# Another way to compute the modulation in the first loop of a transformer-layer kernel: scale columns with the weights as moving operand, shift and gate as VectorE dot products

## The chip, the cores and the metric

The kernel runs on one core of a Trainium2 chip. Its engines have instruction queues of their own and meet at semaphores: TensorE (PE in the profile, with PEld for the loading of its stationary operand), VectorE (DVE), ScalarE (ACT), GpSimd (POOL) and SyncE (SP), which issues most DMAs. The metric is the device time of one execution in microseconds. Three runs of the kernel before took 1252.56, 1253.64 and 1255.13 us; their median, 1253.64, is the time before.

## What is computed

One layer of a diffusion backbone over 512 latent and 256 context tokens with D = 1024: a half-step SwiGLU network, token mixing (attention and a chunked gating network side by side), and a second SwiGLU network. The change is in the first of the three. Cut down to what matters:

```python
def modulate(h, shift, scale):
    return h * (1 + scale) + shift

def swiglu(h, w1, w3, w2):
    return (jax.nn.silu(h @ w1) * (h @ w3)) @ w2

def ffn_sublayer(h_in, shift, scale, gate, norm_w, w1, w3, w2):
    h = modulate(rms_norm(h_in, norm_w), shift, scale)
    return h_in + 0.5 * gate * swiglu(h, w1, w3, w2)

mx = jnp.split((jax.nn.silu(c) @ w_ada + b_ada)[:, None, :], N_MOD, axis=-1)
mc = jnp.split((jax.nn.silu(c_ctx) @ w_ada + b_ada)[None, None, :], N_MOD, axis=-1)
x = ffn_sublayer(x, mx[0], mx[1], mx[2], norm1_w, ffn1_w1, ffn1_w3, ffn1_w2)
ctx = ffn_sublayer(ctx, mc[0], mc[1], mc[2], norm1_w, ffn1_w1, ffn1_w3, ffn1_w2)
```

`w_ada` is 1024 by 9216: nine vectors of 1024 (shift, scale, gate for each sublayer), for two conditions, `c` for latent tokens and `c_ctx` for context tokens.

## The kernel before

Everything is kept transposed: a tile has 128 features on its partitions and tokens in its columns. `x` is 8 blocks of 128 features by 768 tokens (two groups of 256 latent and 128 context tokens). To reach fp32 accuracy at the speed of the reduced type, each operand is split into a high and a low half (`split`, `operand`: ScalarE casts the high half, VectorE subtracts it for the low half), and each product is three matmuls, high by high, high by low, low by high (`mm3`).

**Head.** `x` is loaded, ScalarE squares it, VectorE adds up the squares, and a matmul with ones (L407) gives the sum over features, from which `r` and `v` make the reciprocal root (`rs`). Columns of `w_ada` come as `block` tiles, 1 MB each: shift and scale of 128 features. `ada_mm` (L219) multiplies them with `sc`, silu of the two conditions: the weights are the stationary operand, and two columns move. For each feature block `ada_first` runs 16 of these (8 for the scale, 8 for the shift), and `ada_fin` turns the result into `a` = (1 + scale) times the norm weight, and `s`, the shift.

**First loop, over the 8 feature blocks k.** For block k VectorE multiplies `x` by `a` and `rs` (`first_x`, into a short-lived tile `xa`), ScalarE adds the shift into `hh`, VectorE makes the low half `hl`, and TensorE adds block k to the first two f's (`NFIRST`) of the up projection: 12 matmuls of 512 latent columns (L373). The context part follows some steps behind (`first_ctx`, 12 matmuls of 256 columns, L429). In this loop `nc.ordered` is set and matmuls are pinned, so VectorE, ScalarE, GpSimd and TensorE run in the order of the code; elsewhere a scheduler sets the order, and instructions that are not pinned may be put between. Only two `block` buffers exist, so the load for step k+2 waits for a block to be read.

**Plain up projections, f = 2 to 5 (`NPLAIN1` = 6).** `up1` runs 96 matmuls of 384 columns per f (L125 to L127). After f = 2, 3 and 4, `ada_gate` computes gates as `ada_mm` does. Meanwhile GpSimd prepares the sums of token blocks that the next stage needs (`diff`, `less`, L648 to L654), out of the high and low halves; they are split into T2, T3 and T4 as the scheduler finds room, and T1, which takes the place of a block that the plain projections still read, last.

**f = 6 to 21 by a seven-product scheme (`Winograd`).** Per f, 84 matmuls instead of 96; GpSimd forms sums of weights, VectorE sums of products. Between its parts `ada_step` computes the remaining vectors of `w_ada`, now on VectorE: `ada_dot` multiplies a tile of 128 by 1024 with `cb`, the condition laid out along the columns on all partitions, and accumulates along the row. `cb` is loaded by two DMAs that broadcast (`cvec`) and passed through silu (L469). The down projections (`down`) of five chunks of f's are put in after f = 5, 6, 10, 14 and 18, and the sixth follows the stage.

Of the kernel before, what the change touches and what calls it, by code (L numbers as in the profile page):

```python
# [31 lines left out]
LAG = 2  # L32
NPLAIN1 = 6
NPLAIN2 = 2
BLOCKS = 2
RAWS = 3
OPS = 5
# [93 lines left out]
def layer_kernel(ctx: ExitStack, tc: tile.TileContext, xT, cvec, wfirst, wst, wada, wuq, wkpe, cols, wrope, vnw, rope, out):  # L131
# [27 lines left out]
    sc = const.tile([P, NK, 2], F32, name="sc")  # L159
    epsc = const.tile([P, 1], F32, name="epsc")  # L160
# [26 lines left out]
    gp = fctx.enter_context(tc.tile_pool(name="ffn1g", bufs=2))  # L187
    sctx = ExitStack()
# [10 lines left out]
    def first_units(k):  # L199
        r, rw = st.block(wada, k), st.raw()  # L200
        nc.sync.dma_start(rw[:, :W1], wfirst[k])
        return r, rw

    units = [first_units(0)]
    for k in range(0, NK, 4):
        load_x(k, 4, slice(256, 384))
    units.append(first_units(1))
# [7 lines left out]
    between = []  # L215

    def ada_mm(pt, r, later=False):
        for kt in range(NK):
            f = lambda kt=kt: pin(nc.tensor.matmul(pt, r[:, kt * P : kt * P + P], sc[:, kt, :], start=kt == 0, stop=kt == NK - 1))  # L219
            between.append(f) if later else f()  # L220

    def ada_dot(raw, c, which):
# [3 lines left out]
        nc.vector.scalar_tensor_tensor(  # L226
            out, raw, 1.0, cb[:, which, :], ALU.mult, ALU.mult,
            accum_out=acc[which][:, c : c + 1],
        )
# [92 lines left out]
    class SsqAcc:  # L322
# [4 lines left out]
        def add(self, dt, x0):  # L327
# [25 lines left out]
    def rstd_start(which, pt):  # L353
# [12 lines left out]
    class Mixed:  # L366


        def __init__(self):
            self.tensor = self  # L370

        def matmul(self, *a, **k):
            pin(nc.tensor.matmul(*a, **k))  # L373
# [28 lines left out]
    ada_first(units[0][0], 0)  # L402
    sa = None
    for k in range(NK):
        sa = add_sq(sa, k, square0(0, k), nc.vector)
    sumx = mm()
    pin(nc.tensor.matmul(sumx, ones, sa, start=True, stop=True))  # L407
# [975 lines left out]
```

## Time and profile before

| | before |
|---|---|
| median of three runs | 1253.64 us |
| profiled execution, own time | 1256.85 us |
| its span, first to last instruction | 1255.1 us |
| TensorE busy | 1200.2 us (96%) |
| VectorE busy | 911.1 us (73%) |
| ScalarE busy | 532.7 us (42%) |
| GpSimd busy | 474.8 us (38%) |
| mean granted TensorE clock | 0.974 |
| chain that ended last | PE 76%, DVE 12%, POOL 3%, ACT 3%, DMA 3%, issue 3% |

The profiled execution is one run, 3.2 us above the median of the three; times inside it are counted from the start of its span. A busy TensorE is not TensorE at its peak: a matmul that runs at half clock counts as busy for twice as long, and one of two columns as much as its weights take to load. The part of the program that the change touches ends at about 240 us. What lies behind it, up to 1255.1, is the rest of the first network, token mixing and the second network.

### The profile page before, as it was taken

To read this page: it belongs to the slowest core of one execution; us is meant where nothing else is said; L and a number is where in the kernel's file an instruction comes from. 1 tells how busy PE (TensorE), PEld (TensorE's weight loads), DVE (VectorE), ACT (ScalarE), POOL (GpSimd) and SP (SyncE) were. 2 spreads that over 40 slices of the span, in tenths; PEclk is the share of its full clock that TensorE was granted. 3 is DMA by queue.
4 is the path that set the end of the run, shared out by engine and by line. 5 is a ranking of instruction groups with operands and counts; after the bars stand their busy time and mean duration, and the time that the engine had idled before them with its cause. 6 is when DMAs were issued, how large, how long until landed. Compare 5 with 4: busy or idle time off the path is not lost.

```text
span 1255.1 us, 19295 instructions
## 1 busy us (share of the span) xinstructions
PE 1200.2 (96%) x7266; PEld 1134.5 (90%) x7266; DVE 911.1 (73%) x1607; ACT 532.7 (42%) x1057; POOL 474.8 (38%) x435
## 2 busy tenths in 40 slices
PE   6999899998999999999999999999789999999998
PEld 6888899998999999999978878998778989999997
DVE  3445426889896787876884697776998777778784
ACT  3233222323324324323654455997554444444442
POOL 0328701123213214231541762887573434343330
PEclk9889889999999999999998999999899999999999
DMA  7443232334362372433413311002304132413212
GB/s 256 140 151 110 74 127 80 118 97 147 132 216 103 102 229 74 135 130 101 134 55 114 95 57 51 2 1 66 103 35 134 68 135 68 134 69 135 84 51 84
DMA packets 36093, 131.69 MB, mean 105 GB/s; under 512 B 3744, under 2 KB 10656, under 8 KB 30368
## 3 DMA queue, kind: packets, MB, share of 16 engines
q1 hardware_dynamic: 35568, 129.35, 31.2%
q8 instruction: 57, 0.93, 0.3%
q10 hardware_dynamic: 432, 1.11, 0.3%
q14 instruction: 36, 0.29, 0.1%
HBM read 128.35 MB, written 2.10 MB: 104 GB/s over the span
## 4 chain that ended last, share of the span: by engine, by line
PE 76%; DVE 12%; POOL 3%; ACT 3%; DMA 3%; issue 3%; SPq 0%; DVEq 0%; POOLq 0%; ACTq 0%
PE mm L125 15%; PE mm L126 15%; PE mm L127 15%; PE big L125 8%; PE big L126 7%; PE big L127 7%; PE mm L219 4%; DVE opl L103 3%; PE big L373 2%; DVE junk L226 1%; DMA raw<-wst 1%; PE mm L1060 1%; DMA block<-wada 1%; DVE x L314 1%; PE mm L1075 1%
## 5 line engine op out<-in xcount | busy, mean ns | idle before, releaser
L102 ACT CAST oph<-block 128x512 fp32r<-128x512 f32 x216 | 133.9, 621 | 242.8 <-PE mm L126 159.6
L103 DVE TENSOR_TENSOR opl<-block,oph 128x512 fp32r<-128x512 f32 x216 | 190.9, 887 | 36.8 <-ACT oph L102 36.2
L125 PE MATMUL mm<-gh,oph 128*128 128x384 f32 (+2 forms) x532 | 186.9, 353 | 4.0 <-DVE x L314 2.8
L127 PE MATMUL mm<-gh,opl 128*128 128x384 f32 (+2 forms) x532 | 186.1, 352 | 1.4 <-DVE opl L103 1.4
L126 PE MATMUL mm<-gl,oph 128*128 128x384 f32 (+2 forms) x532 | 187.0, 351 | 0.0
L103 DVE TENSOR_TENSOR opl<-raw,oph 128x512 fp32r<-128x512 f32 x162 | 129.3, 804 | 51.4 <-ACT oph L102 51.2
L102 ACT CAST oph<-raw 128x512 fp32r<-128x512 f32 x162 | 98.6, 618 | 150.8 <-PE mm L126 72.3
L571 POOL TENSOR_TENSOR block<-block 128x512 f32<-128x512 f32 x36 | 48.9, 1358 | 243.3 <-DVE opl L103 243.3
L555 POOL TENSOR_TENSOR s<-block 128x512 f32<-128x512 f32 x36 | 54.6, 1518 | 159.3 <-DMA block<-wst 66.0
L125 PEld LDWEIGHTS mm<-gh,oph 128*128 128x128 f32 x532 | 99.9, 188 | 12.4 <-PE mm L127 2.7
L125 PE MATMUL big<-hh,oph 128*128 128x384 f32 (+1 forms) x288 | 99.3, 345 | 11.7 <-DVE sl L308 5.2
L127 PEld LDWEIGHTS mm<-gh,opl 128*128 128x128 f32 x532 | 99.8, 188 | 8.7 <-DVE opl L103 2.0
L126 PEld LDWEIGHTS mm<-gl,oph 128*128 128x128 f32 x532 | 99.9, 188 | 6.6
L127 PE MATMUL big<-hh,opl 128*128 128x384 f32 (+1 forms) x288 | 98.8, 343 | 0.7 <-DVE opl L103 0.7
L126 PE MATMUL big<-hl,oph 128*128 128x384 f32 (+1 forms) x288 | 98.7, 343 | 0.0
L570 POOL TENSOR_TENSOR block<-s,block 128x512 f32<-128x512 f32 x36 | 54.2, 1505 | 109.7 <-DVE opl L103 109.0
L314 DVE SCALAR_TENSOR_TENSOR x<-mm,g,x 128x256 f32<-128x256 f32 x206 | 76.4, 412 | 16.6 <-PE mm L127 16.6
L320 DVE SCALAR_TENSOR_TENSOR x<-mm,g,x 128x512 f32<-128x512 f32 x55 | 41.0, 749 | 49.9 <-PE mm L127 49.8
L125 PEld LDWEIGHTS big<-hh,oph 128*128 128x128 f32 x288 | 56.7, 197 | 13.3 <-DVE sl L308 6.3
L569 POOL TENSOR_TENSOR block<-block 128x512 f32<-128x512 f32 x36 | 57.5, 1599 | 2.6
L127 PEld LDWEIGHTS big<-hh,opl 128*128 128x128 f32 x288 | 56.2, 195 | 1.6 <-DVE opl L103 1.4
L126 PEld LDWEIGHTS big<-hl,oph 128*128 128x128 f32 x288 | 56.4, 196 | 0.1
(497 smaller groups left out, 3446.3 us busy)
## 6 DMA issues: line engine op xcount, KB each, us to landing
raw<-wst SPq DMA_DIRECT2D x86, 512.0 KB, 4.0
block<-wst SPq DMA_DIRECT2D x36, 1024.0 KB, 4.9
raw<-wada SPq DMA_DIRECT2D x56, 512.0 KB, 4.2
block<-wada SPq DMA_DIRECT2D x8, 1024.0 KB, 5.0
x<-xT SPq DMA_DIRECT2D x6, 512.0 KB, 6.6
raw<-wfirst SPq DMA_DIRECT2D x8, 256.0 KB, 3.8
out<-x SPq DMA_DIRECT2D x7, 256.0 KB, 2.1
cb<-cvec ACTq DMA_DIRECT2D x2, 512.0 KB, 6.7
```

The costliest lines, as they stand in the source:

```text
L102: self.nc.scalar.copy(dst[0], src)
L103: (eng or self.nc.vector).tensor_sub(dst[1], src, dst[0].bitcast(F32))
L125: nc.tensor.matmul(out, lh, rh, start=first, stop=False, skip_group_check=more)
L126: nc.tensor.matmul(out, lh, rl, start=False, stop=False, skip_group_check=more)
L127: nc.tensor.matmul(out, ll, rh, start=False, stop=last, skip_group_check=more)
L219: f = lambda kt=kt: pin(nc.tensor.matmul(pt, r[:, kt * P : kt * P + P], sc[:, kt, :], start=kt == 0, stop=kt == NK - 1))
L314: nc.vector.scalar_tensor_tensor(x[:, dt, s0 : s0 + sn], pt[:, o : o + sn], mod_g[i][which][:, dt : dt + 1], x[:, dt, s0 : s0 + sn], ALU.m ...
L320: nc.vector.scalar_tensor_tensor(lat(x, dt), two(pt), mod_g[i][0][:, dt : dt + 1], lat(x, dt), ALU.mult, ALU.add)
L555: nc.gpsimd.tensor_add(s1, q[2], q[3])
L569: nc.gpsimd.tensor_sub(q[2], q[0], q[2])
L570: nc.gpsimd.tensor_sub(q[0], s1, q[0])
L571: nc.gpsimd.tensor_sub(q[1], q[1], q[0])
```

## The change

1. **Condition by broadcast matmuls.** The loads of `cvec` go. Sixteen matmuls with `sc` broadcast as the stationary operand and the identity as the moving one lay the condition out along the columns in PSUM, and ScalarE copies it to `cb` (`put_cb`). Four more matmuls with ones (`WARM`) follow.
2. **Scale with moving weights.** `ada_row` makes `sc` (two columns) the stationary operand and moves the weights, 128 columns at a time: 8 matmuls give the scale as a row, ScalarE copies it (`row`), and `ada_col` turns it into a column with one matmul.
3. **Shift and gate as dots.** `ada_shift` computes the shift of each block by two `ada_dot`s (one for each condition), and the gates are done by `ada_step` after f = 2 and 3.
4. **A step ahead.** In step k the code prepares `x`, `hh` and `hl` of k+1 and the modulation of k+2. There is a third `block` buffer, in the pool of the loop, and the first steps of the context part are set by a table (`ctx_h`).
5. **Kept h.** `first_x` writes into `hf`, which holds all of h in fp32. The token-block differences are made of it, one subtraction each, on VectorE (L663 to L668), instead of `diff` and `less` on GpSimd.
6. **`NPLAIN1` from 6 to 4.** f = 4 and 5 move from the plain form to the seven-product one.
7. Smaller: epsilon is the bias of the reciprocal root and is added in the steps behind it, so that the instructions that added it to the squares go; `w_ada` is laid out in another way on the host; a scratch size is set.

```diff
-NPLAIN1 = 6
+NPLAIN1 = 4
+WARM = 4
...
+    def ada_row(r, d):
+        o = pa[0:2, (d % 2) * P : (d % 2) * P + P]
+        for kt in range(NK):
+            pin(nc.tensor.matmul(o, sc[:, kt, :], r[:, kt * P : kt * P + P], start=kt == 0, stop=kt == NK - 1))
+        row = sp.tile([2, P], F32, tag="row", name=f"row_{d}")
+        nc.scalar.copy(row, o)
+        return row
+
+    def ada_col(row, d):
+        o = pa[:, 256 + 2 * d : 258 + 2 * d]
+        pin(nc.tensor.matmul(o, row, ident[0:2, 0:2], start=True, stop=True))
         nc.vector.tensor_scalar(
-            pairs[0][1][:, d, :], pa[:, 16 + 2 * d : 18 + 2 * d], b1[:, NK + d : NK + d + 1],
-            col[:, COL_N1 + d : COL_N1 + d + 1], ALU.add, ALU.mult)
-        nc.vector.tensor_scalar_add(pairs[0][0][:, d, :], pa[:, 2 * d : 2 * d + 2], col[:, d : d + 1])
+            pairs[0][1][:, d, :], o, b1[:, NK + d : NK + d + 1], col[:, COL_N1 + d : COL_N1 + d + 1], ALU.add, ALU.mult)
+
+    def ada_shift(r, d, alone=False):
+        for which in range(2):
+            ada_dot(r[:, D:], d, which, accs[:, d, which : which + 1])
+            if alone:
+                nc.vector.tensor_add(mod_s[0][which][:, d : d + 1], accs[:, d, which : which + 1], col[:, d : d + 1])
+            yield
+        if not alone:
+            nc.vector.tensor_scalar_add(pairs[0][0][:, d, :], accs[:, d, :], col[:, d : d + 1])
...
+    def first_h(k, which):
+        sel = parts[which][0]
+        nc.scalar.activation(sel(hf, k), sel(hf, k), AF.Identity, bias=mod_s[0][which][:, k : k + 1])
+        nc.scalar.copy(sel(hh, k), sel(hf, k))
...
     pa = mm()
-    ada_first(units[0][0], 0)
+    bb = [big() for _ in range(2)]
+    for w in range(2):
+        for kt in range(NK):
+            pin(nc.tensor.matmul(bb[w][:, kt // 4, (kt % 4) * P : (kt % 4) * P + P], sc[:, kt, w : w + 1].to_broadcast([P, P]), ident,
+                                 start=kt % 4 == 0, stop=True, skip_group_check=True))
+    for i in range(WARM):
+        pin(nc.tensor.matmul(two(warm[:, :256]), ones, ones2, start=True, stop=True))
...
+    ctx_h = {2: (0, 1), 3: (2, 3), 4: (4,), 5: (5,), 6: (6, 7)}
     for k in range(NK):
...
+        later = k + 2 < NK
+        shift = ada_shift(units[k + 2][0], k + 2) if later else iter(())
+        if k + 1 < NK:
+            first_x(k + 1, 0)
+            ops[k + 1] = st.operand(units[k + 1][1][:, :W1])
+            first_h(k + 1, 0)
+            next(shift, None)
+            first_l(k + 1, 0)
...
         for i in range(2 * NFIRST):
...
+            first_mm(k, i)
+        if later:
+            row = ada_row(units[k + 2][0], k + 2)
+        next(shift, None)
...
     def after1(f):
-        if f < NPLAIN1 - 1:
-            for d in range(3 * (f - NFIRST), min(NK, 3 * (f - NFIRST) + 3)):
-                ada_gate(d)
+        if f < NPLAIN1:
+            for _ in range(4):
+                ada_step()
...
             for i in range(4):
...
+                b11, b12, b21, b22 = (half(k0, g0, i) for k0 in (0, 4) for g0 in (0, 384))
+                nc.vector.tensor_sub(tmps[i], b12, b11)
+                nc.vector.tensor_sub(b12, b22, b12)
+                split([b[:, i, :] for b in blocks["T3"]], b12)
+                nc.vector.tensor_sub(b22, b22, tmps[i])
+                split([b[:, i, :] for b in blocks["T2"]], b22)
+                nc.vector.tensor_sub(b21, b21, b22)
+                split([b[:, i, :] for b in blocks["T4"]], b21)
```

The order of the instructions shows what moves. On TensorE, at the program's start, before:

```order
L211 MATMUL mm_129<-ones 128x256 x3
L219 MATMUL mm_137<-sc,block_115 128x2 x16
L407 MATMUL mm_179<-sq_00_154,ones 128x512
L219 MATMUL mm_137<-sc,block_123 128x2 x16
L219 MATMUL mm_137<-sc,block_211 128x2 x16
L373 MATMUL big_207<-hh,oph_219 128x512
```

And TensorE at the same place in the changed program (the numbers stand for buffers; `sq_00` is the sum of squares, `big_150` and `big_152` the broadcast condition, block_120 and block_126 the first two blocks of weights):

```order
L215 MATMUL mm_140<-ones 128x256 x3
L391 MATMUL big_150<-ident,sc 128x128 x8
L391 MATMUL big_152<-ident,sc 128x128 x8
L394 MATMUL mm_140<-ones 128x256 x4
L402 MATMUL mm_199<-sq_00_173,ones 128x512
L253 MATMUL mm_148<-block_120,sc 2x128 x8
L260 MATMUL mm_148<-ident,row_212 128x2
L253 MATMUL mm_148<-block_126,sc 2x128 x8
L260 MATMUL mm_148<-ident,row_246 128x2
L441 MATMUL big_258<-hh,oph_225 128x512
```

The sum of squares no longer stands behind matmuls that read a block of weights, and the third block's have moved behind the first 12 matmuls of the loop. On VectorE, one step of the loop without a context part, before (`mm_137` holds the modulation, `xa_0_1` is `x` scaled in block 1):

```order
L57 TENSOR_SCALAR a_75<-mm_137,b_73,col 128x2
L57 TENSOR_SCALAR s_74<-mm_137,col 128x2
L57 SCALAR_TENSOR_TENSOR xa_0_1_274<-x,a_75,v_198 128x512
L57 TENSOR_TENSOR opl_279<-raw_126,oph_277 128x512
L57 SCALAR_TENSOR_TENSOR hl<-xa_0_1_274,s_74,hh 128x2x256
```

And VectorE in the changed program, the step k = 0, which prepares block 1 and the shift of block 2 (block_134):

```order
L57 TENSOR_SCALAR a_75<-mm_148,b_73,col 128x2
L57 SCALAR_TENSOR_TENSOR hfull<-x,a_75,v_202 128x2x256
L57 TENSOR_TENSOR opl_271<-raw_129,oph_269 128x512
L57 SCALAR_TENSOR_TENSOR junk_277,accs<-block_134,cb 128x1024
L57 TENSOR_TENSOR hl<-hfull,hh 128x2x256
L57 SCALAR_TENSOR_TENSOR junk_303,accs<-block_134,cb 128x1024
L57 TENSOR_SCALAR s_74<-accs,col 128x2
```

Two dots of 128 by 1024 have come in, one of them ahead of the low half `hl`. On VectorE again, in f = 2, where gate dots (`raw_995`, `raw_1004`) have been put among other work; `raw_1021` is the first half of f = 3's weights:

```order
L223 SCALAR_TENSOR_TENSOR junk_998,accc<-raw_995,cb 128x1024
L313 TENSOR_TENSOR sl_880<-big_776,sl_880 128x384
L223 SCALAR_TENSOR_TENSOR junk_1001,accx<-raw_995,cb 128x1024
L306 TENSOR_TENSOR gl_772<-sl_880,gh_770 128x384
L103 TENSOR_TENSOR opl_1026<-raw_1021,oph_1024 128x512
L223 SCALAR_TENSOR_TENSOR junk_1007,accc<-raw_1004,cb 128x1024
L103 TENSOR_TENSOR opl_1032<-raw_1021,oph_1030 128x512
```

The low halves of f = 3's operands stand behind six gate dots; before, no dot stood in this part of VectorE's queue.

More of the change, by code (lines that the diff above doesn't have):

```diff
@@ L130, in layer_kernel @@
 @with_exitstack
-def layer_kernel(ctx: ExitStack, tc: tile.TileContext, xT, cvec, wfirst, wst, wada, wuq, wkpe, cols, wrope, vnw, rope, out):
+def layer_kernel(ctx: ExitStack, tc: tile.TileContext, xT, wfirst, wst, wada, wuq, wkpe, cols, wrope, vnw, rope, out):
     nc = Core(tc)
@@ L199, in first_units @@
     def first_units(k):
-        r, rw = st.block(wada, k), st.raw()
+        r, rw = st.block(wada, k, sp if k % 3 == 2 else None), st.raw()
         nc.sync.dma_start(rw[:, :W1], wfirst[k])
         return r, rw
-    units = [first_units(0)]
+    units = [first_units(k) for k in range(2)]
     for k in range(0, NK, 4):
         load_x(k, 4, slice(256, 384))
-    units.append(first_units(1))
+    units.append(first_units(2))
     warm = mm()
@@ L213, in layer_kernel, with ada_dot @@
     nc.scalar.activation(epsc2, sc[:, 0, 0:1], AF.Abs_reciprocal_sqrt, bias=epsc, scale=0.0)
[L215 to L222, printed above, removed]
+    def ada_dot(raw, c, which, to=None):
         out = raw
@@ L227, in ada_dot @@
             out, raw, 1.0, cb[:, which, :], ALU.mult, ALU.mult,
[L228 removed]
+            accum_out=acc[which][:, c : c + 1] if to is None else to,
         )
@@ L405, in layer_kernel @@
         sa = add_sq(sa, k, square0(0, k), nc.vector)
+    put_cb = lambda w: nc.scalar.copy(cb[:, w, :], bb[w].rearrange("p g c -> p (g c)"))
+    put_cb(0)
+    nc.vector.tensor_scalar_add(b1, col[:, COL_B : COL_B + 72], 1.0)
     sumx = mm()
     pin(nc.tensor.matmul(sumx, ones, sa, start=True, stop=True))
-    ada_first(units[1][0], 1)
     r0 = rstd_start(0, sumx)
-    nc.vector.tensor_scalar_add(b1, col[:, COL_B : COL_B + 72], 1.0)
-    ada_fin(0)
+    row = ada_row(units[0][0], 0)
+    shift = ada_shift(units[0][0], 0, True)
+    next(shift)
     rs = [rstd_end(*r0)]
+    ada_col(row, 0)
+    ops = {}
+    first_x(0, 0)
+    ops[0] = st.operand(units[0][1][:, :W1])
+    first_h(0, 0)
+    first_l(0, 0)
+    put_cb(1)
+    for _ in shift:
+        pass
+    row = ada_row(units[1][0], 1)
+    for _ in ada_shift(units[1][0], 1):
+        pass
+    ada_col(row, 1)
     pbs = bigs(4)
@@ L430, in first_ctx, with first_mm @@
                                      skip_group_check=True))
-    ops = {}
-    done = 0
-    for k in range(NK):
-        if k + 2 < NK:
-            units.append(first_units(k + 2))
-        if k:
-            ada_fin(k)
-        v = first_x(k, 0)
-        ops[k] = st.operand(units[k][1][:, :W1])
-        lo = first_l(k, 0, v)
-        next(lo), next(lo, None)
-        if k + 2 < NK:
-            ada_first(units[k + 2][0], k + 2)
-        uh, ul = ops[k]
-        for i in range(2 * NFIRST):
-            c = slice(i * P, i * P + P)
-            mm3(mixed, two(pbs[i]), (uh[:, c], ul[:, c]), (lat(hh, k), lat(hl, k)), k == 0, k == NK - 1)
-        if k < 2:
-            for j in range(4 * k, 4 * k + 4):
+    def first_mm(k, i):
+        uh, ul = ops[k]
+        c = slice(i * P, i * P + P)
+        for m, (l, r) in enumerate(((uh, hh), (uh, hl), (ul, hh))):
+            pin(nc.tensor.matmul(two(pbs[i]), l[:, c], lat(r, k), start=k == 0 and m == 0, stop=k == NK - 1 and m == 2))
+    ctx_h = {2: (0, 1), 3: (2, 3), 4: (4,), 5: (5,), 6: (6, 7)}
+    for k in range(NK):
+        if k + 3 < NK:
+            units.append(first_units(k + 3))
+        later = k + 2 < NK
[6 more added lines that the diff above has]
+            first_l(k + 1, 0)
+        if k == 2:
+            rx = rstd_start(1, sumx)
+            rs.append(rstd_end(*rx))
+            pcs += [mm() for _ in range(NFIRST)]
+        for j in ctx_h.get(k, ()):
+            first_x(j, 1)
+            first_h(j, 1)
+        for i in range(2 * NFIRST):
+            first_mm(k, i)
+        if later:
+            row = ada_row(units[k + 2][0], k + 2)
+        next(shift, None)
+        for j in ctx_h.get(k, ()):
+            first_l(j, 1)
+        for j in ctx_h.get(k - 1, ()):
+            first_ctx(j)
+        next(shift, None)
+        if later:
+            ada_col(row, k + 2)
+        if k == 0:
+            for j in range(NK):
                 sx = add_sq(sx, j, square0(1, j), nc.gpsimd)
```

117 lines of the change are left out of this document (31 added, 86 removed).

## The prediction

> **What bounds the kernel now.** I read the windows view first, cut at the marks that the change touches: the first matmul of the loop over k (34.91), the first plain matmul of f=2 (99.57), 197.10, where all but 24 matmuls of f=5 are done and `down` chunk 0 is under way, and the first matmul of `down` chunk 1 (237.69). Columns: start:end, length, busy time and count of PE, PEld, DVE, ACT, POOL, granted clock, DMA share, GB/s.
>
> ```profile
> core 0: us, PE busy (x) PEld busy (x) DVE busy (x) ACT busy (x) POOL busy (x), PEclk, DMA share, GB/s
> 0.00:34.91 34.91, 25.27 (x104) 23.11 (x105) 10.27 (x21) 11.47 (x21) 3.44 (x9) 1.00 0.73 243
> 34.91:99.57 64.66, 63.84 (x355) 56.62 (x355) 32.69 (x62) 19.48 (x37) 16.51 (x18) 0.84 0.46 159
> 99.57:197.10 97.53, 89.34 (x496) 87.48 (x497) 37.42 (x52) 24.30 (x45) 47.13 (x43) 0.88 0.28 90
> 197.10:237.69 40.59, 40.59 (x235) 40.59 (x234) 33.27 (x67) 12.08 (x22) 6.82 (x5) 1.00 0.27 91
> 237.69:500.00 262.31, 255.66 (x1449) 252.90 (x1449) 220.35 (x398) 83.67 (x155) 68.57 (x44) 1.00 0.42 138
> 280.00:320.00 40.00, 35.68 (x202) 35.04 (x201) 40.00 (x63) 14.22 (x27) 17.77 (x10) 1.00 0.39 132
> ```
>
> TensorE bounds the stage up to 237.69, but badly used: 35 us pass before the loop, the loop runs at 0.84 of the clock, f=2 to 5 at 0.88. VectorE is half idle there (32.69 of 64.66, 37.42 of 97.53). Behind it TensorE works at full clock, and only 280:320 is VectorE's (40.00 of 40). So a gain must come ahead of 237.69. The timeline shows the head:
>
> ```profile
> 1.04 2.93 PE L211 MATMUL mm<-ones 128*128 128x256 f32 x6 [1.04 <-DVE nhalf L167]
> 7.14 4.67 DVE L57 TENSOR_TENSOR sq<-sq,sq 128x512 f32<-128x512 f32 x6 [0.18 <-ACT sq L57]
> 12.07 6.96 PE L219 MATMUL mm<-sc,block 128*128 128x2 f32 x32 [8.11 <-DMA block<-wada]
> 18.89 2.05 PE L407 MATMUL mm<-sq,ones 128*128 128x512 f32 x2
> 20.74 6.83 PE L219 MATMUL mm<-sc,block 128*128 128x2 f32 x32
> 20.98 0.60 ACT L57 ACTIVATE r<-mm 128x512 f32<-128x512 f32 x1 [10.10 <-PE mm L407]
> 27.60 0.28 DVE L57 TENSOR_SCALAR a<-mm,b,col 128x2 f32<-128x2 f32 x1 [15.69 <-PE mm L219]
> 29.37 0.69 DVE L57 SCALAR_TENSOR_TENSOR v<-v,r 128x512 f32<-128x512 f32 x1
> 30.09 0.75 DVE L57 SCALAR_TENSOR_TENSOR xa<-x,a,v 128x512 f32<-128x512 f32 x1
> 30.76 0.68 DVE L57 TENSOR_TENSOR opl<-raw,oph 128x512 fp32r<-128x512 f32 x1
> 31.63 0.75 DVE L57 SCALAR_TENSOR_TENSOR hl<-xa,s,hh 128x512 fp32r<-128x512 f32 x1 [0.19 <-ACT hh L57]
> 34.91 0.77 PE L373 MATMUL big<-hh,oph 128*128 128x512 f32 x1
> ```
>
> The squares are summed at 11.81, yet their matmul (L407) stands behind 32 passes of L219 until 18.89; the scale `a` waits 15.69 us for the next 32, and the first loop matmul stands behind a third 32. Three times 7 us of two-column matmuls are the head.
>
> **Part 1, the head.** Removed ahead of L407: one L219 group. Added: 16 broadcast matmuls of 128 columns and 4 of 256. A 128x256 fp32 matmul is two passes of 2.93/6 = 0.49 us; halved, the 16 cost 7.8 us, the 4 cost 3.9. From 3.97 that ends at 15.7 if the clock stays as it is in that row. The loop's rows show what full-width work does to it:
>
> ```profile
> 38.47 0.63 PE L373 MATMUL big<-hh,opl 128*128 128x512 f32 x1
> 38.90 0.63 PE L373 MATMUL big<-hh,oph 128*128 128x512 f32 x1
> 39.91 4.01 PE L219 MATMUL mm<-sc,block 128*128 128x2 f32 x32
> 57.10 0.39 PE L373 MATMUL big<-hh,oph 128*128 128x512 f32 x1
> 57.33 0.40 PE L373 MATMUL big<-hl,oph 128*128 128x512 f32 x1
> 57.81 0.28 PE L429 MATMUL mm<-hh,oph 128*128 128x256 f32 x1
> 57.93 0.28 PE L429 MATMUL mm<-hl,oph 128*128 128x256 f32 x1
> ```
>
> Slots (start to start) are 0.43 us at the low rate, 0.23 and 0.12 at the full one, and the rise comes between 38.90 and 39.91, after 4 to 5 us of such work. Here work begins at 1.04, so I take the rise at 5.5 and the end of the added matmuls near 11: bounds 11 and 15.7, the first taken. L407's successor then starts at 11.8, with the squares, and takes 1.0. Behind it: r 0.6, three v steps of 0.72 (29.37 to 30.09), a, x, the operand's low half, now two ScalarE passes (0.72 and 0.6), the low half `hl`: 18.7. The first loop matmul also waits for the second copy to `cb` (half of 1.92, row below), the copy of `row` and its transposing matmul (no row shows them; between nothing and the 0.6 of r, 0.3 taken): **19.9 instead of 34.91, a gain of 15.0** (11 with the low rate). Block 0 is no limit: it was there at 12.07, and the DMA order ahead of it is unchanged.
>
> **Part 2, the loop.** TensorE does 96 matmuls at 0.23 and 96 at 0.12, 33.6 us; and six times the scale. For the scale with 128 moving columns the trace has no row. Bounds: the same weights as stationary operand were 32 passes in 4.01 us for two kinds, so 2.0 for one; and 16 passes at half of the 0.49 above are 3.9 at the low rate, 2.0 at the full one. I take 1.9, 11.4 in all, for the full rate (3.9 is in the rival below). Sum 45. VectorE gets the dots:
>
> ```profile
> L226 DVE SCALAR_TENSOR_TENSOR junk<-raw,cb x32: 1204/1212/2310, 203.9 to 342.9; 128x1024 bf16<-128x1024 f32 x32
> 203.85 1.22 DVE L226 SCALAR_TENSOR_TENSOR junk<-raw,cb 128x1024 bf16<-128x1024 f32 x1
> 205.00 0.08 DVE L226 DVE_READ_ACCUMULATOR junk<-raw,cb 128x1 f32 x1
> 205.00 0.69 DVE L103 TENSOR_TENSOR opl<-raw,oph 128x512 fp32r<-128x512 f32 x1
> 205.61 0.73 DVE L314 SCALAR_TENSOR_TENSOR x<-mm,g,x 128x256 f32<-128x256 f32 x2
> L57 DVE SCALAR_TENSOR_TENSOR xa<-x,a,v 128x256 f32<-128x256 f32 x8 | 3.8, 478 | 0.0
> L533 DVE TENSOR_TENSOR hl<-tt,hh 128x384 fp32r<-128x384 f32 x4 | 2.1, 556 | 1.2 <-ACT hh L532 1.2
> L103 DVE TENSOR_TENSOR opl<-block,oph 128x512 fp32r<-128x512 f32 x96 | 79.4, 831 | 19.2 <-ACT oph L102 19.1
> L469 ACT ACTIVATE cb<-cb 128x2048 f32<-128x2048 f32 x1 | 1.9, 1922 | 3.8 <-DMA cb<-cvec 3.8
> ```
>
> A dot holds VectorE from 203.85 to 205.00, 1.15 us; an operand's low half 0.61, the x step 0.67. From the first `hl` at 18.7 to the evacuation that frees the banks for f=2, VectorE's order has 15 dots (17.3), 7 x steps (4.7), 10 operand halves (6.5), 7 `hl` (4.9), 15 context steps at 0.45 (6.8), 18 differences and splits of 384 columns at 0.5 (9.0), small ones and the evacuation (5.0): 53.2. That is more than TensorE's 45: **the bound of the loop changes from TensorE to VectorE.** With 3 us for waits, f=2 starts at 75 instead of 99.57: the loop takes 55 instead of 64.66. By full durations (dot 1.29, the others 0.06 more each) it is 79; TensorE alone would give 65.
>
> The Trainium skill, "Vector Engine (DVE) Microarchitecture Reference", section "Points that are easy to get wrong", says that this form with two non-bf16 SBUF sources halves throughput. Both inputs of the dot are fp32 in SBUF, and its median of 1.212 us is no slower per element than the 0.69 of a 512-column subtraction; the trace does not agree. By the rule a dot would be nearer 2.3 us and this loop 17 us longer.
>
> **Part 3, f=2 to `down` chunk 1.** Removed: 64 gate matmuls (the three L219 rows below, 16.2 us of TensorE), and POOL's difference chain, which kept 47 us busy and which the splits waited for. Moved: f=4 and 5 from 96 matmuls to 84 each.
>
> ```profile
> 117.70 6.77 PE L219 MATMUL mm<-sc,raw 128*128 128x2 f32 x48
> 126.73 0.69 PE L125 MATMUL big<-hh,oph 128*128 128x384 f32 x1 [2.26 <-ACT oph L102]
> 150.81 5.84 PE L219 MATMUL mm<-sc,raw 128*128 128x2 f32 x48
> 178.04 3.63 PE L219 MATMUL mm<-sc,raw 128*128 128x2 f32 x32
> raw<-wada SPq DMA_DIRECT2D x56, 512.0 KB, 4.2
> ```
>
> By the changed order TensorE has 576 matmuls of 384 columns up to the first of `down` chunk 1. At 40.59/235 = 0.173 they take 99.6, with the last context matmuls 101, where it was 138.1. VectorE on the way: in f=2 and 3, 16 gate dots (18.4) and everything else about 17, 35 us beside TensorE's 36; the four splits of T1 then stand behind the last gate dots and f=3's own matmuls, 2 us of wait. In f=4 and 5, 12 dots (13.8), 14 operand halves at 0.83 (11.6), 13 steps of 0.55 and two small ones (7.9), and 2 us left over, 35 against TensorE's 153 x 0.173 = 26.5: 8 us of wait. Chunk 0 has slack again. 101 + 10 + 2 for what interlocks: **113 instead of 138.1, a gain of 25** (bounds 101 and 120). What is late next is the operand halves behind the dots, not the DMAs: each half lands in 4.2 us and there are three buffers.
>
> After that the order of all engines is nearly the same, so I count nothing for f=6 on. The other edits (epsilon in the bias instead of an added step, fewer POOL steps on squares, the `cvec` loads gone) save under 1 us on the chain.
>
> Sum: 15.0 + 9.7 + 25 = 49.7; I take 49. The profiled execution took 1256.85 us (span 1255.1), so 1208; the median, 1253.64, is 3.2 lower: **1205**.
>
> **Rivals.** *Fuller durations*: the dots and the neighbours cost their whole durations, or the low clock holds in the broadcasts; f=2 at 79, third part 118, head 4 later: gain 36 to 41, 1212 to 1218. For it: everything hangs on one in-order queue. Against: the slots at 203.85 to 205.61.
>
> *Better packed*: the waits of parts 2 and 3 vanish; VectorE's own sums remain (53 and 35 and 35): gain 55 to 60, 1194 to 1199.
>
> *Half clock*: TensorE, now waiting, falls to the low rate for the loop: 45 becomes 86, f=2 at 106, gain 19, 1235. Against: 280:320 has TensorE waiting in the same way, at 1.00.
>
> *Slower than before*: the dots, in VectorE's order ahead of the operand halves that TensorE needs, run like the worst of their row, 2.310 with 0.08 for the accumulator. 43 dots stand ahead of `down` chunk 1; each costs 1.24 more, 53 us together, and the kernel ends at 1258. It decides from 2.29 us per dot. For it: the maximum exists. Against: the median, and POOL, whose steps could collide, is left with little up to f=4.
>
> The Trainium skill, "SBUF — State Buffer", section "Who interferes with whom", has VectorE instructions with two SBUF inputs and GpSimd ones that read SBUF lock each other out for a whole instruction; the 2.310 fits it, and the change takes POOL's chain away from the dots.
>
> **How the numbers follow.** Forecast 0.55 (1199 to 1211), fuller durations 0.30, better packed 0.07, half clock 0.05, slower 0.03. From 1194 to 1224 about 0.9 lies, and no bound above asks for less on either side. A measurement of this kernel tells about 0.2% (2.5 us) from no change. Faster 0.96, same 0.01, slower 0.03.
>
> **What would show it.** First loop matmul near 20 and L402 near 12; f=2 near 75, with VectorE over 90% busy in the loop and a clock near 1.00; dots at 1.2 us; `down` chunk 1 near 188. Wrong if TensorE is still the busy engine in the loop, if the dots exceed 1.4, or if 237.69's gain is given back in f=6 to 9.

## The result, and the profile after

| | before | after |
|---|---|---|
| median | 1254.35 us (4 runs) | 1215.24 us (4 runs, 1211.91 to 1216.12) |
| ratio to before, 95% interval | | 0.9685 (0.9664 to 0.9707) |
| profiled execution, its span | 1256.85, 1255.1 us | 1216.12, 1214.0 us |
| first matmul of the loop over k | 34.91 | 19.79 |
| first plain matmul, f=2 | 99.57 | 77.31 |
| first matmul of `down` chunk 1 | 237.69 | 194.12 |
| from there to the end of the span | 1017.4 | 1019.9 |

The change saves 39 us, 10 less than forecast; 1215 lies inside the stated range and outside the likeliest case (1199 to 1211). The windows view of the kernel after, cut at its own marks (start:end, length, busy time and count of PE, PEld, DVE, ACT, POOL, granted clock, DMA share, GB/s):

```profile
0.00:19.79 19.79, 14.87 (x84) 11.19 (x84) 11.53 (x23) 13.21 (x22) 0.68 (x6) 1.00 0.97 324
19.79:77.31 57.52, 50.19 (x292) 38.78 (x292) 54.35 (x107) 31.21 (x68) 8.87 (x7) 0.97 0.56 201
77.31:115.00 37.69, 36.79 (x214) 36.47 (x215) 36.69 (x68) 13.44 (x29) 3.17 (x3) 1.00 0.46 153
115.00:150.00 35.00, 25.42 (x138) 23.18 (x136) 35.00 (x47) 11.63 (x22) 14.51 (x9) 0.99 0.29 97
150.00:194.12 44.12, 44.12 (x239) 44.12 (x240) 36.74 (x79) 10.65 (x19) 6.17 (x4) 0.93 0.39 140
235.00:275.00 40.00, 32.13 (x170) 31.81 (x169) 36.26 (x58) 12.69 (x24) 13.27 (x9) 0.87 0.46 158
...
77.31:194.12 116.81, 106.33 (x588) 103.77 (x589) 108.42 (x192) 35.72 (x69) 23.86 (x15) 0.97 0.38 131
```

VectorE is busy 54.35 of 57.52 us in the loop and 35.00 of 35 in f=4 and 5 (115 to 150), where TensorE stands still for 9.6 us. Between them, in f=2 and 3, both engines are full. The mark that was expected at 75 came at 77.31, and the stage behind it took 116.8 us, not 113. The head, in the timeline (start, duration, engine, line, tiles, idle time before and its releaser):

```profile
3.90 4.71 PE L391 MATMUL big<-ident,sc 128*128 128x128 f32 x32
8.45 1.89 PE L394 MATMUL mm<-ones 128*128 128x256 f32 x8
11.96 1.12 PE L402 MATMUL mm<-sq,ones 128*128 128x512 f32 x2 [1.62 <-DVE sq L57]
13.02 1.91 PE L253 MATMUL mm<-block,sc 128*2 128x128 f32 x16
18.40 0.69 DVE L57 TENSOR_TENSOR hl<-hfull,hh 128x512 fp32r<-128x512 f32 x1 [0.83 <-ACT hh L57]
19.48 0.38 PE L260 MATMUL mm<-ident,row 2*128 2x2 f32 x2 [1.34 <-ACT row L57]
19.79 0.50 PE L441 MATMUL big<-hh,oph 128*128 128x512 f32 x1
```

The sum of squares (L402) now waits for the squares and nothing else. The broadcasts and the four `WARM` matmuls end at 10.34, and TensorE then idles 1.62 us. The scale of one block with moving weights took 1.91 us for its 16 passes.

In the loop, VectorE's and GpSimd's rows around 30 us show what the forecast had not counted:

```profile
29.63 1.21 DVE L57 TENSOR_TENSOR opl<-raw,oph 128x512 fp32r<-128x512 f32 x1
30.76 1.75 DVE L57 SCALAR_TENSOR_TENSOR junk<-block,cb 128x1024 bf16<-128x1024 f32 x1
32.44 1.20 DVE L57 TENSOR_TENSOR hl<-hfull,hh 128x512 fp32r<-128x512 f32 x1
33.56 1.74 DVE L57 SCALAR_TENSOR_TENSOR junk<-block,cb 128x1024 bf16<-128x1024 f32 x1
...
26.54 9.34 POOL L57 TENSOR_TENSOR sq<-sq,sq 128x256 f32<-128x256 f32 x7 [25.25 <-ACT sq L57]
```

Beside GpSimd's seven sums of context squares, a dot takes 1.75 us and a subtraction of 512 columns 1.21; alone they take 1.22 and 0.69 (rows of e1, below). The waits view of the loop (total, times, longest) puts 3.9 us of TensorE's idle time to the finished sum, in one wait, with the next steps' matmuls queued behind it:

```profile
PE mm L479 <- POOL sq L57: 3.9, 1, 3.9
```

### The profile page after: what moved, and what is told of

Its sections match the earlier page's. It is cut to its first block, busy times and chain, and to the rows that moved or that the text cites. A ratio compares the mean times of both kernels' runs of the same rounds, so it can differ in the third digit from the quotient of the medians.

```text
span 1214.0 us, 18922 instructions
## 1 busy us (share of the span) xinstructions
PE 1149.2 (95%) x7042; PEld 1078.5 (89%) x7042; DVE 963.5 (79%) x1699; ACT 545.4 (45%) x1090; POOL 422.6 (35%) x388
## 4 chain that ended last, share of the span: by engine, by line
PE 70%; DVE 14%; ACT 3%; issue 2%; DMA 1%; POOL 0%; DVEq 0%; POOLq 0%; ACTq 0%
PE mm L125 15%; PE mm L126 15%; PE mm L127 15%; PE big L125 7%; PE big L126 7%; PE big L127 7%; DVE opl L103 4%; DVE junk L223 1%; PE mm L1064 1%; DMA raw<-wada 1%; DVE x L319 1%; DVE hh L301 1%; PE mm L1079 1%; PE mm L1080 1%; DVE hl L302 1%
## 5 line engine op out<-in xcount | busy, mean ns | idle before, releaser
L102 ACT CAST oph<-block 128x512 fp32r<-128x512 f32 x228 | 141.3, 621 | 250.8 <-PE mm L126 167.2
L103 DVE TENSOR_TENSOR opl<-block,oph 128x512 fp32r<-128x512 f32 x228 | 209.3, 922 | 36.4 <-ACT oph L102 35.6
L587 POOL TENSOR_TENSOR block<-block 128x512 f32<-128x512 f32 x38 | 51.6, 1357 | 258.3 <-DVE opl L103 231.0
L103 DVE TENSOR_TENSOR opl<-raw,oph 128x512 fp32r<-128x512 f32 x154 | 119.2, 779 | 19.6 <-ACT oph L102 19.4
L125 PE MATMUL big<-hh,oph 128*128 128x384 f32 (+1 forms) x240 | 79.8, 333 | 9.6 <-DVE gl L306 7.9
L126 PE MATMUL big<-hl,oph 128*128 128x384 f32 (+1 forms) x240 | 79.8, 333 | 0.0
L127 PE MATMUL big<-hh,opl 128*128 128x384 f32 (+1 forms) x240 | 79.6, 332 | 0.0
L223 DVE SCALAR_TENSOR_TENSOR junk<-raw,cb 128x1024 bf16<-128x1024 f32 x48 | 63.1, 1315 | 1.7 <-DMA raw<-wada 1.3
L585 POOL TENSOR_TENSOR block<-block 128x512 f32<-128x512 f32 x38 | 60.3, 1588 | 2.8
L127 PE MATMUL mm<-hh,opl 128*128 128x384 f32 x160 | 54.0, 337 | 3.0 <-DVE opl L103 3.0
L126 PE MATMUL mm<-hl,oph 128*128 128x384 f32 x160 | 54.6, 341 | 2.2 <-DVE hl L302 2.2
```

The lines of the kernel that those rows point to most:

```text
L102: self.nc.scalar.copy(dst[0], src)
L103: (eng or self.nc.vector).tensor_sub(dst[1], src, dst[0].bitcast(F32))
L125: nc.tensor.matmul(out, lh, rh, start=first, stop=False, skip_group_check=more)
L126: nc.tensor.matmul(out, lh, rl, start=False, stop=False, skip_group_check=more)
L127: nc.tensor.matmul(out, ll, rh, start=False, stop=last, skip_group_check=more)
L223: nc.vector.scalar_tensor_tensor(out, raw, 1.0, cb[:, which, :], ALU.mult, ALU.mult, accum_out=acc[which][:, c : c + 1] if to is None else to,
```

## The experiments

My theory was that VectorE's in-order queue decides everything from 19.8 to 194 us, that GpSimd's two-input steps lengthen VectorE's, and that the 10 missing us are such collisions and TensorE's waits for operand halves behind dots. Every kernel is the changed one with one edit, unless said otherwise. Each is compared with the kernel before on its own chip. "Loop" is from the first loop matmul to f=2, "stage" from there to `down` chunk 1, both of the profiled run.

| run | median us | ratio, 95% interval | loop | stage | rest of span |
|---|---|---|---|---|---|
| changed kernel | 1215.24 | 0.9685 (0.9664 to 0.9707) | 57.5 | 116.8 | 1019.9 |
| e12: the same again | 1215.35 | 0.9674 (0.9654 to 0.9695) | 58.5 | 115.5 | 1021.3 |
| e1: context squares on TensorE | 1213.0 | 0.9663 (0.9640 to 0.9686) | 55.0 | 115.3 | 1020.4 |
| e2: late dots | 1203.76 | 0.9594 (0.9568 to 0.9620) | 58.7 | 104.9 | 1017.5 |
| e3: scale with stationary weights | 1212.67 | 0.9660 (0.9637 to 0.9683) | 54.6 | 116.5 | 1019.1 |
| e4: shift dots twice | 1229.22 | 0.9795 (0.9772 to 0.9817) | 71.6 | 116.1 | 1017.5 |
| e5: gates on TensorE | 1230.35 | 0.9795 (0.9774 to 0.9816) | 57.6 | 131.0 | 1019.2 |
| e6: no `WARM` matmuls | 1216.49 | 0.9683 (0.9657 to 0.9710) | 58.7 | 115.1 | 1017.0 |
| e7: differences on GpSimd | 1216.78 | 0.9695 (0.9667 to 0.9723) | 59.1 | 116.1 | 1020.0 |
| e8: late dots, f=4 and 5 plain | 1209.18 | 0.9620 (0.9597 to 0.9643) | 58.8 | 112.1 | 1017.8 |
| e9: late dots, spread | 1214.03 | 0.9663 (0.9640 to 0.9687) | 58.3 | 106.4 | 1029.3 |
| e10: e9 and e1 | 1210.77 | 0.9634 (0.9613 to 0.9654) | 55.0 | 104.7 | 1029.1 |
| e11: e9, e1 and e3 | 1204.41 | 0.9586 (0.9567 to 0.9605) | 51.2 | 105.5 | 1024.2 |

Eight runs with the loop's dots, sums and scale as changed (e7 among them, with the differences on GpSimd) took 57.5 to 59.1 us for it, so a loop shorter by 3 us is more than scatter, though the whole time hardly tells it.

**e1, the sums of context squares.**

```diff
-                sx = add_sq(sx, j, square0(1, j), nc.gpsimd)
+                sqs.append(square0(1, j))
...
-            pin(nc.tensor.matmul(sumx, ones, sx, start=True, stop=True))
+            for j in range(NK):
+                pin(nc.tensor.matmul(sumx, ones, sqs[j], start=j == 0, stop=j == NK - 1))
```

> The context columns' squares are summed by eight accumulating ones-matmuls on TensorE instead of seven additions on POOL and one matmul; all other engines keep their order. Theory (POOL's additions and VectorE hold each other up in the loop): POOL has nothing to do before 77 us, the dots at 30 to 36 us fall from 1.75 to 1.2 us, TensorE's 3.9 us wait for the sum at 36 goes, f=2 starts at 73 to 74.5 instead of 77.31, and the time is 1211 to 1213 (after: 1215.2). Rival (those dots are long because of the DMAs that run then, or the loop is late elsewhere): dots stay above 1.6 us, f=2 at 76.5 to 79, time 1214 to 1217, with about 2 us more TensorE work.

The windows view over the loop, and two rows of VectorE at the same place:

```profile
20.58:75.56 54.98, 51.55 (x307) 40.28 (x306) 51.29 (x107) 31.42 (x68) 0.00 (x0) 1.00 0.59 205
...
30.30 1.22 DVE L57 SCALAR_TENSOR_TENSOR junk<-block,cb 128x1024 bf16<-128x1024 f32 x1
31.44 0.69 DVE L57 TENSOR_TENSOR hl<-hfull,hh 128x512 fp32r<-128x512 f32 x1
```

The same 107 VectorE steps take 51.29 us instead of 54.35, the dots are back at 1.22, and the wait for the sum is gone. In the stretch of the long dots, 30.3 to 36, the DMA share is 0.82 in this run and was 0.43 in the changed kernel, so DMAs do not lengthen the dots. f=2 came at 75.56, between the theory's range and the rival's: the loop began 0.8 us later, and is 2.5 us shorter. The edit also takes away TensorE's 3.9 us wait; in e3 below that wait stays (3.7 us) while VectorE is busy 54.14 of 54.56, so it is VectorE's time that counts. The theory holds for the mechanism; the gain in the whole time, 2 us, is within the intervals.

**e2, late dots.**

```diff
+    skip = 6
+    def wino_step():
+        nonlocal skip
+        skip -= 1
+        if skip < 0:
+            ada_step()
...
-    Winograd(gp, 384, U_UP1, blocks, g_tile, 1).run(NPLAIN1, after1, ada_step)
+    Winograd(gp, 384, U_UP1, blocks, g_tile, 1).run(NPLAIN1, after1, wino_step)
```

> The first six modulation dots-steps of the seven-product form (those in f=4 and 5) are left out there, and all 48 steps stand in f=6 to 21, one in each slot. Theory (VectorE's queue bounds 115 to 150, where it is busy 35.0 of 35): VectorE loses 12 dots of 1.2 to 2.3 us there, the 9.2 us that TensorE waits for operands at L127 fall to 1 to 3, `down` chunk 1 starts at 186 to 188 instead of 194.12, and since VectorE has slack later (30 to 33 of 40 us) the time is 1208 to 1210. Rival (the wait is only moved: the dots come back where `down` chunks load VectorE, as at 235 to 275): chunk 1 as early, but the time is 1213 to 1217. A second rival (the wait in f=4 and 5 is for operand latency, not for the dots): chunk 1 at 192 to 195.

The windows view of that run:

```profile
78.41:115.00 36.59, 35.69 (x208) 35.37 (x209) 35.78 (x67) 12.45 (x27) 2.42 (x2) 1.00 0.48 155
115.00:150.00 35.00, 33.17 (x190) 32.56 (x189) 30.09 (x42) 13.80 (x27) 13.86 (x10) 1.00 0.23 79
150.00:183.27 33.27, 33.27 (x193) 33.27 (x192) 27.72 (x59) 8.87 (x16) 5.53 (x4) 1.00 0.34 112
```

The wait for operand halves in 115 to 150, first of the changed kernel, then of e2:

```profile
PE mm L127 <- DVE opl L103: 7.8, 4, 3.2
```

```profile
PE mm L127 <- DVE opl L103: 1.2, 1, 1.2
```

TensorE's idle time in 115 to 150 falls from 9.6 to 1.8 us, its busy time in the stage from 106.3 to 102.1, and chunk 1 starts at 183.27. The run is 11.5 us faster than the changed kernel, more than any theory gave, and its interval lies below that of the changed kernel. Dots in f=4 and 5 were the wait. Why the gain exceeds the idle time saved stands under the clock, below.

**e3, the scale as before.**

```diff
-        o = pa[0:2, (d % 2) * P : (d % 2) * P + P]
+        o = pa[:, 256 + 2 * d : 258 + 2 * d]
         for kt in range(NK):
-            pin(nc.tensor.matmul(o, sc[:, kt, :], r[:, kt * P : kt * P + P], ...))
-        row = sp.tile([2, P], F32, tag="row", name=f"row_{d}")
-        nc.scalar.copy(row, o)
-        return row
+            pin(nc.tensor.matmul(o, r[:, kt * P : kt * P + P], sc[:, kt, :], ...))
+        return o
```

(`ada_col` then reads `o`, without a matmul.)

> The scale goes back to the old form: the weights are stationary and the two columns of silu(c) move, with no row copy on ScalarE and no transposing matmul; the shift stays as dots. Theory (the loop is VectorE's, and the scale's form on TensorE costs 2 us a step either way, beside it): first loop matmul at 19.0 to 20.0, f=2 at 76 to 78.5, time 1214 to 1216.5. Rival (the moving form is what keeps the clock up, and the narrow matmuls bring back the 0.84 of the loop before): granted clock in the loop 0.80 to 0.90, f=2 at 81 to 86, time 1219 to 1225.

The windows view over the loop of e3, then the groups over the loop with the step that makes `a`, of the changed kernel and of e3 (out<-in, busy, mean ns, idle before and its releaser):

```profile
20.35:74.91 54.56, 48.57 (x280) 42.18 (x280) 54.14 (x107) 30.00 (x62) 7.91 (x7) 0.91 0.59 207
```

```profile
L57 DVE TENSOR_SCALAR a<-mm,b,col 128x2 f32<-128x2 f32 x7 | 1.9, 274 | 2.4 <-PE mm L260 2.4
```

```profile
L57 DVE TENSOR_SCALAR a<-mm,b,col 128x2 f32<-128x2 f32 x7 | 1.9, 271 | 0.0
```

Both theories missed. The clock does fall, to 0.91, and the loop is still 3 us shorter, because VectorE is the bound: it is busy 54.14 of 54.56, and its 2.4 us of waiting for the transposing matmul L260 are gone. The runs that move the weights, with the same dots and sums, have 0.94 to 0.97 there. The loop does not need it, and moving the weights pays with a longer chain to `a`: matmuls, a copy on ScalarE, another matmul.

**e4, each shift dot twice.**

```diff
+            ada_dot(r[:, D:], d, which, accs2[:, d, which : which + 1])
             ada_dot(r[:, D:], d, which, accs[:, d, which : which + 1])
```

> Every shift dot of the head and the loop is done twice (16 more, the extra result is not used). Theory (VectorE's in-order queue bounds the loop): each costs its slot of 1.15 to 1.25 us, f=2 at 94 to 98 instead of 77.31, time 1232 to 1236. Rival (the loop is bound by TensorE's 50 us of work and VectorE's 54 have room): f=2 at 79 to 86, time 1217 to 1224.

The windows view over the loop:

```profile
21.09:92.71 71.62, 54.83 (x292) 41.68 (x291) 71.20 (x137) 31.16 (x68) 9.00 (x7) 0.88 0.45 155
```

Fifteen more dots in the loop cost 14.1 us there, 0.94 each, and VectorE is full. The rival (f=2 at 79 to 86) falls: f=2 came at 92.71. The theory was 1.15 to 1.25 each, so the 3.2 us in which VectorE waited took up the difference; f=2 and the time, 1229.2, lie just under the theory's 94 and 1232.

**e5, the gates on TensorE.**

```diff
-            for _ in range(4):
-                ada_step()
+            for d in range(4 * (f - NFIRST), 4 * (f - NFIRST) + 4):
+                ada_gate(d)
...
-    ada_next = 2 * NK
+    ada_next = 3 * NK
```

(`ada_gate` as in the kernel before, and its layout of the weights.)

> The eight gates go back to TensorE (64 matmuls of two moving columns in f=2 and 3, with one small VectorE step each) in place of the 16 gate dots. Theory (in f=2 and 3 both engines are nearly full, so the 16.2 us that these matmuls took in the kernel before come on top of TensorE's 101, while the 18.4 us of dots that go only take the waits behind them): f=2 to `down` chunk 1 takes 120 to 126 instead of 116.8, time 1218 to 1224. Rival (VectorE alone sets this stage, and TensorE has the room): 112 to 117, time 1210 to 1215.

The group of the gates, and the windows view over f=2 to 5:

```profile
L277 PE MATMUL mm<-sc,raw 128*128 128x2 f32 x128 | 21.0, 301 | 0.0
```

```profile
78.09:115.00 36.91, 36.19 (x206) 35.87 (x207) 17.15 (x32) 9.56 (x20) 4.31 (x3) 0.86 0.29 100
115.00:150.00 35.00, 34.27 (x183) 33.95 (x182) 21.22 (x36) 9.17 (x18) 6.91 (x4) 0.80 0.34 106
```

TensorE is the bound again, busy 98% of the time at a clock of 0.80 to 0.86, and VectorE is busy for 46 and 61%. The gates take 21.0 us, not 16.2, and the neighbours run slower too: the stage takes 131 us, 14.2 more, where 3 to 9 were expected. The direction was right, the price too small: the low clock comes with these matmuls and was not in it. Doing the gates as dots is worth 14 to 15 us.

**e6, without `WARM`.**

```diff
-WARM = 4
+WARM = 0
```

> The four 256-column matmuls behind the broadcasts (whose result is not used) are left out. Theory (they end 1.6 us before the squares' sum, and only fill TensorE's wait): first loop matmul at 19.5 to 20.7, time 1213.5 to 1216.5. Rival (they keep the clock up over the wait): the passes of the first two scales run at twice their length, first loop matmul at 21.5 to 24, time 1217 to 1219.

The scale's passes in that run's timeline:

```profile
13.67 1.91 PE L253 MATMUL mm<-block,sc 128*2 128x128 f32 x16
```

The passes take the same 1.91 us, the loop begins at 20.44 (20.46 to 20.58 in e1, e5, e9 and e10, whose sum of squares came as late), and the time is the same. The four matmuls do nothing that can be measured.

**e7, the token differences on GpSimd.**

```diff
-                nc.vector.tensor_sub(tmps[i], b12, b11)
+                nc.gpsimd.tensor_sub(tmps[i], b12, b11)
```

(and the three others likewise.)

> The 16 token differences are made by POOL instead of VectorE, still one step each from the kept h. Theory (POOL's and VectorE's steps of two inputs hold each other up): VectorE is rid of 8.8 us, but its neighbours get longer by about as much (dots of 1.7 to 2.3 us beside the differences) and the splits wait for POOL; `down` chunk 1 at 191 to 198, time 1212 to 1219. Rival (POOL is a free engine): VectorE's queue is 8 us shorter, chunk 1 at 185 to 188, time 1206 to 1209.

The windows view, loop and stage:

```profile
19.86:78.93 59.07, 51.16 (x292) 39.39 (x292) 55.18 (x95) 31.46 (x68) 23.17 (x19) 0.94 0.55 195
78.93:195.01 116.08, 105.51 (x590) 104.23 (x589) 108.86 (x188) 35.90 (x69) 30.51 (x20) 0.96 0.39 132
```

VectorE has 16 instructions less, 283 for 299, and is busy 164.0 us for 162.8: what left it came back as longer neighbours. GpSimd works 21 us more. The time is unchanged, as the theory had it, and the rival (8 us faster) falls. So the time does not show which engine subtracts. That it is the kept fp32 copy of h that makes the differences cheap, one step each instead of two or three, is not tested: no run makes them in the old way.

**e8, late dots with f=4 and 5 plain.**

```diff
-NPLAIN1 = 4
+NPLAIN1 = 6
...
-        if f < NPLAIN1:
+        if f < 4:
             for _ in range(4):
```

> f=4 and 5 go back to the plain form (96 matmuls each instead of 84), with the gate dots in f=2 and 3 and all 48 later dots in f=6 to 21, so it stands against the run with late dots (1203.8). Theory (without dots in f=4 and 5 TensorE bounds them, at 33.2 of 35 us there): 24 matmuls of 0.173 come back, time 1207 to 1209, and 6 to 8 us better than after. Rival (VectorE still bounds the seven-product form there): 1202 to 1205.

1209.2, 0.2 above the theory's range, and a stage 7.2 us longer than in e2: 24 matmuls at 0.173 are 4.2 of it, and in the rest falls a wait of 2.63 us at 113.17, with matmuls at half rate behind it. In this stage the seven-product form takes less time from f=4 on once no dots stand there; the intervals of the two whole times just overlap.

**e9 to e11, the dots spread.** In e2 the first steps, of two dots, come three to an f.

```diff
+        n = 0 if f < 2 else (1, 0, 1)[pos] if f < 10 else (1, 1, 2)[pos]
+        for _ in range(n):
+            ada_step()
```

(f = 0 stands for f=4 here, and pos is the place within f.)

> As the run with late dots, but spread: two steps in each f from 6 to 13 (their steps have two dots), four in each f from 14 to 21 (one dot each), so every f has four dots instead of six and then three. Theory (what is left of the waits behind `down` chunk 1 is VectorE's queue with six dots an f): TensorE's 3.6 us wait behind `gl` near 240 and the clock of 0.83 there go, time 1199 to 1202 against 1203.8. Rival (those waits come from POOL's and VectorE's two-input steps together, whatever the count of dots): 1202.5 to 1205. A second rival (the dots that are added at the end meet the norm behind f=21): 1204 to 1207.

> The same, and the context columns' squares summed on TensorE. Theory (the edits are in different stages and add up): 2 to 3 us less than with the spread dots alone, 1196.5 to 1199.5. Rival (the 2 us were the scatter of runs): no difference over 1 us.

> The same two, and the scale with stationary weights. Theory (the moving form's row copy and transposing matmul make VectorE wait 2.4 us in the loop, and this stays so without POOL's sums): f=2 at 72 to 73.5, time 1194 to 1197.5. Rival (once POOL is out, the lower clock of the narrow matmuls bounds the loop): f=2 at 74.5 to 78, time 1197.5 to 1201.

e9 took 1214.0, 10 us more than e2; of its profiled run, whose span is 13.7 us longer than e2's, 11.8 are in the rest of the span. No theory had this. The windows view of the dots alone (VectorE busy and count in them, an accumulator read beside each; clock, DMA share, GB/s), first of e2, then of e9:

```profile
315.00:355.00 40.00, 2.43 (x4) 1.00 0.38 128
355.00:395.00 40.00, 7.06 (x11) 1.00 0.41 141
395.00:435.00 40.00, 8.28 (x14) 1.00 0.44 149
435.00:475.00 40.00, 4.37 (x6) 1.00 0.33 111
```

```profile
315.00:355.00 40.00, 15.42 (x20) 0.91 0.45 145
355.00:395.00 40.00, 4.93 (x8) 1.00 0.40 128
395.00:435.00 40.00, 15.29 (x24) 0.91 0.66 214
435.00:475.00 40.00, 0.00 (x0) 1.00 0.26 89
```

The code gives every f four dots; the schedule that was built bunches them, 15 us in one stretch of 40 and none in another. Where they bunch TensorE waits, and it is busy 34.5 and 36.1 of 40 us in these two stretches, at a clock of 0.91. Its longest wait is near 340, for `gl`:

```profile
PE big L125 <- DVE gl L306: 5.5, 1, 5.5
```

So dots spread in the code were not spread in time, and the expectation was about a schedule that did not run. That the bunching is the cause is read from this trace; no run changes it alone.

On that base e1 and e3 can still be read in the loop, which is the same code: 58.3, then 55.0 with e1, then 51.2 with both. The two gains of 3.3 and 3.8 us add up, and the rivals of e10 and e11 fall (f=2 of e11 came at 71.56, for 72 to 73.5). The expected times, taken from a base that came 12 us late, were all missed. e11's time falls by 6.4 us; 2.6 of that lies outside the loop and is not explained. The three edits that help, e1, e2 and e3, were not run together without the spread.

> The changed kernel, unaltered, for the comparison on the same chip: 1213 to 1217, ratio to the kernel before 0.967 to 0.970.

It gave 1215.35, with a ratio of 0.9674, inside the interval of the first comparison.

## Why the prediction was right, and where it fell short

The sign, the order of the parts and the bound in each were right; the forecast of 1205 was 10 us low, and the time left its likeliest case, 1199 to 1211. None of the three signs that would have made it wrong came: VectorE, not TensorE, is the full engine of the loop (94%), its dots have a median of 1.218 us, and what lies behind `down` chunk 1 did not give the gain back.

- **Part 1, the head.** Forecast 19.9, gain 15.0; measured 19.79 and 15.1. L402 came at 11.96 for 11.8, the added matmuls ended at 10.34 for "near 11": the passes of the broadcasts come 0.21 us apart up to 5.74 and 0.11 from there, where the step took the rise at 5.5. Runs with this head begin the loop between 19.7 and 20.6.
- **Part 2, the loop.** That the bound passes to VectorE is shown by e4. The steps that were listed for it add up to 54.2, not 53.2 (and the rival's 79, with the same 3 us of waits, to some 81). Measured from the end of the first `hl` at 19.09 to f=2, VectorE was busy 54.8 us and waited 3.4, so the waits had the right size; 2.4 of them are the chain to `a` (e3). That the sum came so near is in part luck: undisturbed, in e1, the same steps take 51.8, so they were put too long, and the 3.1 us by which POOL's sums stretch them (e1) were put at nothing. The prediction took POOL's chain of differences out of the way and overlooked that the seven sums now stand beside the dots. The loop took 57.5 us for 55; with the sums and the chain removed, 51.2 (e11).
- **Part 3.** Forecast 113 as 101 of TensorE, 10 of waits, 2 more; measured 116.8 as 106.3 and 10.5. The waits were right, and were dots in f=4 and 5, as said (e2). The term that failed is TensorE's own 101: after a wait its matmuls run at half rate. Without the waits it measured 102.1 (e2).
- **The gates.** Taking them off TensorE was put at 16.2 us of its time; e5 says 14 to 15 us of the end, and that their low clock goes along with them.
- **From f=6 on**, counted nothing; the rest of the span is 2.5 us longer. The runs whose code behind the loop is the same (the changed kernel, twice, e1, e3, e4 and e6) took 1017.0 to 1021.3 there, so this is scatter as far as the runs tell. The wait near 250 (32.13 of 40 us busy) has a smaller counterpart before, at 280 to 320 (35.68 of 40).
- **Rivals.** The time fell into *fuller durations*, 1212 to 1218, but not by its mechanism: a dot that no GpSimd step meets still takes its slot of 1.15 us. *Half clock* was true in pieces, behind long waits, one of them in the loop (below); the loop's mean clock is 0.97. *Slower*: single dots of 2.31 us do occur, the one at 139.42 beside two GpSimd steps (138.97 to 142.85), but the median stayed that of the trace before. *Better packed*: its 1194 to 1199 was reached by no run; the stage of e2 and the loop of e11, by further edits, come to what it describes.

The Trainium skill, "SBUF — State Buffer", section "Who interferes with whom", has VectorE steps with two SBUF inputs and GpSimd steps that read SBUF contend, under an exclusive lock. e1 and e7 agree: 8.87 us of GpSimd cost VectorE 3.06 us, and 21 us of it cost about what 16 subtractions take.

## What to carry to other kernels

When work moves to an engine that becomes the bound, price it with what will run beside it, not with its undisturbed duration, and look for two-input steps on GpSimd there. A higher clock is not worth a longer chain where TensorE waits anyway. Which stretch of time a step lands in decides its price: read it from the schedule that was built, not from the count in the loop.

## What had not been expected of the hardware

A long wait of TensorE mostly costs more than itself. The timeline of the changed kernel shows three waits of over 3 us in the first network; its windows view (columns as above) shows the granted clock behind the first and around the second:

```profile
35.93 0.70 PE L479 MATMUL mm<-sq,ones 128*128 128x256 f32 x2 [3.90 <-POOL sq L57]
149.86 0.69 PE L127 MATMUL mm<-gh,opl 128*128 128x384 f32 x1 [3.19 <-DVE opl L103]
256.00 0.69 PE L125 MATMUL big<-hh,oph 128*128 128x384 f32 x1 [7.87 <-DVE gl L306]
256.48 0.52 PE L126 MATMUL big<-hl,oph 128*128 128x384 f32 x1
```

```profile
35.90:41.00 5.10, 5.07 (x15) 3.81 (x16) 4.96 (x12) 1.72 (x3) 0.00 (x0) 0.67 0.72 257
...
145.00:150.00 5.00, 1.22 (x6) 0.58 (x4) 5.00 (x10) 2.40 (x5) 0.00 (x0) 0.91 0.20 38
150.00:155.00 5.00, 5.00 (x16) 5.00 (x17) 5.00 (x10) 0.96 (x2) 0.00 (x0) 0.50 0.93 365
155.00:160.00 5.00, 5.00 (x28) 5.00 (x27) 3.17 (x9) 0.82 (x2) 0.00 (x0) 0.90 0.32 126
160.00:165.00 5.00, 5.00 (x31) 5.00 (x30) 4.59 (x9) 1.04 (x2) 0.00 (x0) 1.00 0.31 107
```

Behind the second wait 16 and 28 matmuls run in 5 us, then 31 again: 18 slots lost, 3.1 us at 0.173. TensorE counts as busy all that time, which is most of how part 3's 101 became 106. The length of the wait does not decide it alone. In the kernel before, a wait of 3.35 us, in the stretch that the prediction set against *half clock*, left the clock at 1.00:

```profile
293.88 0.45 PE L125 MATMUL big<-hh,oph 128*128 128x384 f32 x1 [3.35 <-DVE gl L301]
...
293.88:299.00 5.12, 5.12 (x29) 5.12 (x30) 5.12 (x8) 2.10 (x4) 3.89 (x3) 1.00 0.53 218
```

The Trainium skill, "TensorE: Matmul & The Clock Gate", section "HAM oscillation — how this bites in real kernels", warns of idle gaps above about 3.4 us; here a gap of 3.19 us, with 1.51 and 0.59 shortly ahead, was enough, and in e8 one of 2.63 us, while the 3.35 us above were not. What decides between them stays open.

And e5 shows the clock at 0.80 to 0.86 with TensorE busy 98% of the time and no wait longer than 0.7 us from 78 to 150: two-column matmuls count as busy in the profile and do not hold the clock.
